# First feed-forward block of an encoder layer: high weights run once over both parts of the input, in another chunk order

## Chip, cores, metric

One NeuronCore of a Trainium2 chip runs the whole kernel. The metric is device time in microseconds (us). The kernel before takes 1095.23 us, the median of three runs.

## What is computed

One encoder layer over 256 tokens of width 2048: windowed attention, a normalisation, and a squared-ReLU network of hidden width 8192, each scaled and shifted by vectors that depend on a conditioning input `c`. The part at issue, cut from the reference:

```python
mod = c_act @ mod_w[i] + mod_b[i]
sh_m, sc_m, g_m, sh_f, sc_f, g_f = jnp.split(mod, 6, axis=-1)
...
hff = x * (1.0 + sc_f[:, None, :]) + sh_f[:, None, :]
u = jnp.square(jax.nn.relu(hff @ w1 + b1))
y = u @ w2 + b2
```

`x` here is the normalised output of the attention part; everything is float32.

## The kernel before

**Products in parts.** TensorE (PE) works on a reduced float32 format. So each operand is split: a high part (a copy in that format) and a low part (the rest). A product is the sum of three: high x high, high weights x low input, low weights x high input. For weights, ScalarE (ACT) makes the high part in L247 and VectorE (DVE) subtracts it from the raw weights in L218, for halves of 1024 columns. The class `Stream` plans all weight loads in one list, issues them on SyncE's queue (SP, L202) into five raw buffers, and keeps five high and five low buffers (`NHIGH`, `NLOW`). `S.main()` hands out the two halves of the next load, `S.done()` gives one half back and prepares further ones.

**The first feed-forward block.** The hidden width is worked off in four blocks of 2048. In blocks 1 to 3 (`ff_hidden`, L983) all 2048 rows of the input are at hand, and the high weights run over 512 columns, both input parts at once (L995), and the low weights over 256 (L996). In block 0 the input is still being made: the 16 slices of 128 rows come in four groups `h2[0]` to `h2[3]`. For that the first matrix is cut into 16 loads of 1 MB (`in_w1a`), here called tiles: tile (kg, fq) has the rows of input group kg and the quarter fq of the block's output columns; it holds 4 x 4 weight blocks of 128x128, that is four *quarters* `fi` of output columns with four slices k each. `W1A` (L470) is the order of the tiles; in that before, kg 0 of two fq, then kg 1 of the same two, and so on. The loop at L955 to L982 does, for each weight block, three products of 256 columns (L971 high x high, L972 high x low, L973 low x high); two quarters share a PSUM bank, one in each half. `psa` has five banks. After kg = 1 the sum of two groups is copied to SBUF by ACT (L977, `uacc`); after kg = 3 DVE adds the second half of the sum to it (L979), and `square_split` (L928) applies bias and ReLU (L934), squares (L936) and splits the result (L937, L938) for the second matrix.

**An input group.** `ff_columns(g)` (L879) needs the scale and shift for four slices: their matrix `in_modf` is multiplied by `c` partly on PE (L307), partly on DVE (L345), both as steps of the same stream; the last step adds the DVE part by PE (L307 with `onesf`), ACT copies the row (L361), two PE transposes (L377) turn it into columns, and DVE computes scale and shift vectors (L383, L384, L885 to L887). `ff_input(g)` (L896) then transposes `x` (L901, two PSUM tiles, two slices each), and for each slice ACT writes the high part (L907), ACT or DVE the full value (L910, L913), and DVE the low part (L915). Groups 1, 2 and 3 are made ahead of tiles 1, 7 and 9; they are used first in tiles 2, 8 and 10.

**Order.** Each engine runs its instructions in one order, which is settled when the kernel is built: a scheduler sorts the instructions as the loops emit them, by their dependences, and moves some past others. On an engine, an instruction that waits holds up what is behind it.

Of the kernel before, what the change touches and what calls it, by code (L numbers as in the profile page):

```python
# [11 lines left out]
F32 = mybir.dt.float32  # L12
F32R = mybir.dt.float32r
I32 = mybir.dt.int32
AF = mybir.ActivationFunctionType
# [5 lines left out]
S = 256  # L21
# [27 lines left out]
def hybrid_kernel(ctx: ExitStack, tc: tile.TileContext, a, out: bass.AP):  # L49
    nc = tc.nc  # L50
    cst = ctx.enter_context(tc.tile_pool(name="cst", bufs=1))
    sml = ctx.enter_context(tc.tile_pool(name="sml", bufs=4))
# [5 lines left out]
    psa = ctx.enter_context(tc.tile_pool(name="psa", bufs=5, space=PSUM))  # L58
# [7 lines left out]
    more = []  # L66
# [7 lines left out]
    def g4(dt=F32):  # L74
        return gen.tile([128, 1024], dt, tag="g4", name="g4")

    def f32(x):
        return x.bitcast(F32)
# [4 lines left out]
    cT, b1 = pack[:, :NK], pack[:, NK:NK + 64]  # L83
# [196 lines left out]
    S = Stream()  # L280
# [155 lines left out]
    for g in range(2, G):  # L436
        n = len(ORDER[g])
# [15 lines left out]
    def plan_late(n):  # L453
        for _ in range(n):
            while lp[0] < len(late) and late[lp[0]].planned == late[lp[0]].n:
                lp[0] += 1
            if lp[0] < len(late):
                late[lp[0]].plan()
# [8 lines left out]
            S.plan(a["wo"][(n - 5) % 4, (n - 5) // 4])  # L467
    S.stop = len(S.q)
    plan_late(4)
    W1A = [(kg, fq) for p in ((0, 1), (2, 3)) for q in ((0, 1), (2, 3)) for kg in p for fq in q]  # L470
    for n, (kg, fq) in enumerate(W1A):
        left = [m.n - m.planned for m, _, _ in m_ff]
        for _ in range(max(W1_FILL[n], left[2] if n == 6 else 0, left[2] + left[3] if n == 8 else 0)):
# [20 lines left out]
    def part(tiles, t, c):  # L494
        return tiles[c][:, t * 512:t * 512 + 512]
# [67 lines left out]
    def qkv(g, ch):  # L563

        _, k0, nk = m_mix[g]
        hh, hl = held[g]
        wh, wl = S.main()
        per = 4 // nk
        for ci in range(per):
            p = ch * per + ci  # L570
            c = CORD[p]
            go_on, held_back = c in half, ((g, ch), p) in CARRY
            pss = half.pop(c, None) or banks()
            for k2 in range(0, nk, 2):
                for t in range(NT):
                    for k in (k2, k2 + 1):
                        s = slice(k * 256 + t * 128, k * 256 + t * 128 + 128)
                        mm3(pss[t], hh[:, s], hl[:, s], wh(ci * nk + k), wl(ci * nk + k),
                            k == 0 and not go_on, k == nk - 1 and not held_back)
                S.done()  # L580
                if per == 1 and k2 == 0:
                    yield
            if held_back:
                half[c] = pss
            else:
                evict(c, pss)
            if per == 2 and ci == 0:
                yield
# [36 lines left out]
    for x, (g, c) in enumerate(qk_order):  # L625
        at = ORDER[g].index(c)
# [207 lines left out]
    for n in range(21):  # L834
        j, i = n // 4, n % 4
# [9 lines left out]
        if n + 1 < len(LATE):  # L845
            w = qkv(*LATE[n + 1])
        else:
            if n == 5:
                ys, bo = [g4b() for _ in range(4)], bias_all(a["bo"], [g4b(), g4b()])
            w = project((n - 5) // 4, (n - 5) % 4)  # L850
# [13 lines left out]
        if n == 9:  # L864

            for c in range(4):
                xs[c] = g4()
                i = nc.gpsimd.dma_start(xs[c].rearrange("p (t n) -> p t n", t=NT), a["x"][:, :, 512 * c:512 * c + 512])
# [12 lines left out]
    def ff_columns(g):  # L881
        m, k0, nk = m_ff[g]
        columns(m, modfb, (scf, shf), k0, nk)
        s = slice(k0, k0 + nk)
        nc.vector.tensor_mul(a2[:, s], lnT[:, 0, s], scf[:, s])  # L885
        nc.vector.tensor_mul(b2[:, s], lnT[:, 1, s], scf[:, s])
        nc.vector.tensor_add(b2[:, s], b2[:, s], shf[:, s])  # L887
# [6 lines left out]
    def ff_input(g):  # L894
        both, hf = [g4(F32R), g4(F32R)], g4()
        for kp in range(2):  # L896
            pt = pst.tile([128, 512], F32, name="pt")
            for i in range(2):
                k = 4 * g + 2 * kp + i
                for t in range(NT):  # L900
                    nc.tensor.transpose(pt[:, i * 256 + t * 128:i * 256 + t * 128 + 128],  # L901
                                        part(xs, t, k // 4)[:, (k % 4) * 128:(k % 4) * 128 + 128], ident)
            for i in range(2):
                k = 4 * g + 2 * kp + i
                s = slice((2 * kp + i) * 256, (2 * kp + i) * 256 + 256)
                hh, hl = (both[kp][:, i * 512 + x * 256:i * 512 + x * 256 + 256] for x in range(2))
                nc.scalar.activation(hh, pt[:, i * 256:i * 256 + 256], AF.Identity,  # L907
                                     scale=a2[:, k:k + 1], bias=b2[:, k:k + 1])
                if i:
                    nc.scalar.activation(hf[:, s], pt[:, i * 256:i * 256 + 256], AF.Identity,  # L910
                                         scale=a2[:, k:k + 1], bias=b2[:, k:k + 1])
                else:
                    nc.vector.tensor_scalar(hf[:, s], pt[:, i * 256:i * 256 + 256], a2[:, k:k + 1],  # L913
                                            b2[:, k:k + 1], op0=OP.mult, op1=OP.add)
                nc.vector.tensor_sub(hl, hf[:, s], f32(hh))  # L915
        return both

    def ff_in(k):

        return h2[k // 4][k % 4 // 2][:, k % 2 * 512:k % 2 * 512 + 512]  # L920

    h2 = [ff_input(0)]
# [2 lines left out]
            normed(c, t)  # L925


    def square_split(ps, ft, n, u, at):  # L928

        rl = sml.tile([128, 512], F32, name="rl", tag="t2", bufs=4)  # L930
        e = n * 256
        for i in range(n):
            s = slice(i * 256, i * 256 + 256)
            nc.scalar.activation(rl[:, s], ps[:, s], AF.Relu, bias=b1[:, ft + i:ft + i + 1])  # L934
        uf = sml.tile([128, 512], F32, name="uf", tag="t2", bufs=4)
        nc.vector.tensor_mul(uf[:, :e], rl[:, :e], rl[:, :e])  # L936
        nc.scalar.copy(u[:, at:at + e], uf[:, :e])  # L937
        nc.vector.tensor_sub(u[:, 512 + at:512 + at + e], uf[:, :e], f32(u[:, at:at + e]))  # L938

    def square_halves(ps, ft, u, at):  # L940

        v = sml.tile([128, 512], F32, name="rl", tag="t2", bufs=4)
        nc.scalar.activation(v[:, 256:], ps[:, 256:], AF.Identity, bias=b1[:, ft:ft + 1])
        nc.vector.tensor_add(v[:, :256], v[:, 256:], ps[:, :256])
        uf = sml.tile([128, 512], F32, name="uf", tag="t2", bufs=4)[:, :256]
        nc.vector.scalar_tensor_tensor(uf, v[:, :256], 0.0, v[:, :256], op0=OP.max, op1=OP.mult)
        h, l = u[:, at:at + 256], u[:, 512 + at:512 + at + 256]
        nc.scalar.copy(h, uf)
        nc.vector.tensor_sub(l, uf, f32(h))

    g2 = None
    uacc = [g4() for _ in range(4)]
    us = []
    opened = {}
    for n, (kg, fq) in enumerate(W1A):  # L955
        if n in (1, 7, 9):
            ff_columns(len(h2))
            h2.append(ff_input(len(h2)))
        wh, wl = S.main()
        for fp in range(2):  # L960
            if kg % 2 == 0:
                opened[fq, fp] = psa.tile([128, 512], F32, name="pa")
            ps = opened[fq, fp]
            for fi in range(2):
                o = ps[:, fi * 256:fi * 256 + 256]
                for k in range(4):
                    w = (fp * 2 + fi) * 4 + k
                    hb = ff_in(4 * kg + k)
                    hh, hl = hb[:, :256], hb[:, 256:]
                    new, end = kg % 2 == 0 and fi + k == 0, kg % 2 == 1 and fi == 1 and k == 3  # L970
                    nc.tensor.matmul(o, wh(w, 128), hh, start=new, stop=False)  # L971
                    nc.tensor.matmul(o, wh(w, 128), hl, start=False, stop=False)  # L972
                    nc.tensor.matmul(o, wl(w, 128), hh, start=False, stop=end)  # L973
            S.done()
            av = uacc[fq][:, fp * 512:fp * 512 + 512]
            if kg == 1:
                nc.scalar.copy(av, ps)  # L977
            elif kg == 3:
                nc.vector.tensor_add(av, av, ps)  # L979
                u = g4(F32R)  # L980
                square_split(av, fq * 4 + fp * 2, 2, u, 0)
                us.append(u)  # L982

    def ff_hidden(blk):
        nonlocal g2
# [40 lines left out]
    for blk in range(BLK - 1):  # L1026
        if blk:
            us = ff_hidden(blk)
# [18 lines left out]
    us = ff_hidden(blk)  # L1047
# [21 lines left out]
    for t in range(NT):  # L1069
        ps = psa.tile([128, 512], F32, name="pa")  # L1070
# [4 lines left out]
        for c in (1, 0, 2, 3):  # L1075
# [8 lines left out]
            q = nc.sync if c % 2 else nc.scalar  # L1084
# [91 lines left out]
```

## Time and profile before

| | us |
|---|---|
| median of three runs | 1095.23 |
| lowest and highest run | 1093.78, 1096.64 |
| profiled execution, first to last instruction (its span; what lies around it is not in the profile) | 1098.2 |
| block 0, first matrix (366.56 to 466.39 in the span) | 99.83 |

Times inside the span are from one profiled execution, whose span is 3.0 us above the median of the runs. Groups are named by line, engine and operation, with output and input names; "x256" is a count, and what follows the last bar is the time that the engine stood idle ahead of the group, with what ended it. In time-ordered lists the first two columns are start and duration in us. PE's recorded durations overlap each other.

### The profile page before, as it was taken

Reading aid. Unit: us, or ns where it says so; the run is one execution under the profiler, and the core shown is the slowest. Engines: PE = TensorE matmul, PEld = TensorE weight load, DVE = VectorE, ACT = ScalarE, POOL = GpSimd, SP = SyncE. Lnnn points to the kernel's source line nnn. Section 1 sums busy time; section 2 is a strip of 40 time slices with the busy share of each in tenths; the row PEclk is TensorE's granted clock in tenths of the full one; section 3 lists DMA queues with packets and bytes.
Section 4 is the critical chain, followed back from the end, with each engine's and each line's share of the span. In section 5 each row is a group of like instructions: output and inputs, shape, how many; then the busy total and the mean of one; then the engine's idle time right before and its main releaser. Section 6 shows DMA issues by size and latency. Waiting matters only on the chain.

```text
span 1098.2 us, 15487 instructions
## 1 busy us (share of the span) xinstructions
PE 1067.6 (97%) x6098; PEld 863.1 (79%) x6098; DVE 804.2 (73%) x1162; ACT 522.0 (48%) x806; POOL 30.0 (3%) x54
## 2 busy tenths in 40 slices
PE   8889999998999999999999999999999999999995
PEld 6657677665677799988888888888888888888884
DVE  4597899978899877754588889756666557665676
ACT  5333346765673537643344543344453334544340
POOL 1000000001000000000000010001000000000001
PEclk9989999999999999999999999999999999999998
DMA  9999987789985996555578788866555555557511
GB/s 384 425 427 425 427 357 280 271 297 379 377 315 201 361 360 244 185 192 192 195 301 303 272 313 306 312 220 225 184 189 190 197 196 186 178 185 267 191 75 77
DMA packets 43337, 292.70 MB, mean 267 GB/s; under 512 B 5104, under 2 KB 5232, under 8 KB 9472
## 3 DMA queue, kind: packets, MB, share of 16 engines
q1 hardware_dynamic: 39312, 279.85, 66.9%
q0 software_dynamic: 3200, 10.50, 2.7%
q10 hardware_dynamic: 752, 1.35, 0.3%
q8 instruction: 48, 0.79, 0.3%
q14 instruction: 25, 0.20, 0.0%
HBM read 289.57 MB, written 2.11 MB: 266 GB/s over the span
## 4 chain that ended last, share of the span: by engine, by line
PE 86%; DVE 7%; DMA 4%; ACT 2%; issue 1%; DVEq 0%; ACTq 0%
PE pa L995 16%; PE pa L500 15%; PE pa L498 15%; PE pa L499 15%; PE pa L996 8%; PE pa L972 3%; PE pa L971 3%; PE pa L973 3%; PE pm L307 3%; DVE wl L218 2%; DMA raw<-in_modm 2%; DMA raw<-in_modf 1%; DVE g L345 1%; DMA raw<-in_wqkv 1%; PE pa L687 1%; PE pa L743 1%
## 5 line engine op out<-in xcount | busy, mean ns | idle before, releaser
L218 DVE TENSOR_TENSOR wl<-raw,wh 128x1024 fp32r<-128x1024 f32 x332 | 403.9, 1223 | 223.6 <-ACT wh L247 222.9
L247 ACT CAST wh<-raw 128x1024 fp32r<-128x1024 f32 x332 | 347.1, 1051 | 441.3 <-PE pa L500 228.6
L498 PE MATMUL pa<-wh,g 128*128 128x512 f32 x816 | 324.1, 398 | 5.1 <-ACT g L519 2.6
L500 PE MATMUL pa<-wh,g 128*128 128x512 f32 x816 | 318.9, 392 | 4.1 <-DVE g L521 3.0
L499 PE MATMUL pa<-wl,g 128*128 128x512 f32 x816 | 320.0, 392 | 0.0
L995 PE MATMUL pa<-g,wh 128*128 128x512 f32 x768 | 270.1, 397 | 0.0
L996 PE MATMUL pa<-g,wl 128*128 128x256 f32 x768 | 214.9, 280 | 0.0
L498 PEld LDWEIGHTS pa<-wh,g 128*128 128x128 f32 x816 | 153.9, 189 | 46.8 <-issue 7.5
L500 PEld LDWEIGHTS pa<-wh,g 128*128 128x128 f32 x816 | 153.5, 188 | 41.2 <-DVE g L521 6.0
L499 PEld LDWEIGHTS pa<-wl,g 128*128 128x128 f32 x816 | 153.9, 189 | 33.0 <-issue 2.4
L995 PEld LDWEIGHTS pa<-g,wh 128*128 128x128 f32 x768 | 144.2, 188 | 36.0 <-issue 0.8
L996 PEld LDWEIGHTS pa<-g,wl 128*128 128x128 f32 x768 | 144.8, 189 | 0.1
L345 DVE SCALAR_TENSOR_TENSOR g<-raw,cact,g 128x1024 f32<-128x1024 f32 x65 | 82.6, 1280 | 2.8 <-DMA raw<-in_modf 2.3
L972 PE MATMUL pa<-g,wh 128*128 128x256 f32 x256 | 72.7, 285 | 0.4 <-DVE g L915 0.4
L971 PE MATMUL pa<-g,wh 128*128 128x256 f32 x256 | 72.5, 286 | 0.0
L973 PE MATMUL pa<-g,wl 128*128 128x256 f32 x256 | 72.3, 283 | 0.0
L307 PE MATMUL pm<-raw,cact 128*32 128x256 f32 (+2 forms) x776 | 48.8, 375 | 5.9 <-DMA raw<-in_modf 3.2
L971 PEld LDWEIGHTS pa<-g,wh 128*128 128x128 f32 x256 | 48.8, 192 | 1.3 <-issue 0.8
L972 PEld LDWEIGHTS pa<-g,wh 128*128 128x128 f32 x256 | 49.1, 192 | 0.9 <-DVE g L915 0.8
L973 PEld LDWEIGHTS pa<-g,wl 128*128 128x128 f32 x256 | 49.1, 192 | 0.0
L345 DVE SCALAR_TENSOR_TENSOR g4b<-raw,cact,g4b 128x1024 f32<-128x1024 f32 x32 | 40.7, 1280 | 9.0 <-DMA raw<-in_modgf 8.8
L307 PEld LDWEIGHTS pm<-raw,cact 128*32 128x32 f32 x776 | 20.9, 112 | 25.9 <-issue 11.5
(165 smaller groups left out, 741.6 us busy)
## 6 DMA issues: line engine op xcount, KB each, us to landing
raw<-in_w SPq DMA_DIRECT2D x64, 1024.0 KB, 4.9
raw<-in_w1b SPq DMA_DIRECT2D x48, 1024.0 KB, 5.0
raw<-in_modm SPq DMA_DIRECT2D x32, 1024.0 KB, 14.8
raw<-in_modf SPq DMA_DIRECT2D x32, 1024.0 KB, 6.9
raw<-in_wqkv SPq DMA_DIRECT2D x24, 1024.0 KB, 12.8
raw<-in_modgm SPq DMA_DIRECT2D x16, 1024.0 KB, 7.5
raw<-in_wo SPq DMA_DIRECT2D x16, 1024.0 KB, 7.5
raw<-in_w1a SPq DMA_DIRECT2D x16, 1024.0 KB, 7.6
```

Source lines behind the costliest of these rows:

```text
L218: self.pinned(nc.vector.tensor_sub(l, r, f32(self.hs[n])))
L247: self.pinned(nc.scalar.copy(h, s))
L307: i = nc.tensor.matmul(self.ps[32 * j:32 * j + 32, :w], lhsT[j] if type(lhsT) is list else lhsT, rhs[j], start=self.first, stop=stop)
L345: nc.vector.scalar_tensor_tensor(p[:, :e], s, cact[:, kt:kt + 1], p[:, :e], op0=OP.mult, op1=OP.add)
L498: nc.tensor.matmul(ps, xh, wh, start=start, stop=False)
L499: nc.tensor.matmul(ps, xh, wl, start=False, stop=False)
L500: S.prev = nc.tensor.matmul(ps, xl, wh, start=False, stop=stop).ins
L971: nc.tensor.matmul(o, wh(w, 128), hh, start=new, stop=False)
L972: nc.tensor.matmul(o, wh(w, 128), hl, start=False, stop=False)
L973: nc.tensor.matmul(o, wl(w, 128), hh, start=False, stop=end)
L995: nc.tensor.matmul(ps, wh(k, 128), hb, start=k == 0, stop=False)
L996: nc.tensor.matmul(ps[:, :256], wl(k, 128), hb[:, :256], start=False, stop=k == NK - 1)
```

## The change

The order of the tiles, the loop over them and the way results leave PSUM are changed; `square_split` goes, and `square_halves`, which blocks 1 to 3 use already, gets a further summand. A quarter of output columns now has a bank of its own: the high weights run over both input parts (512 columns, L957 of the new kernel), the low weights over the high part (256 columns, L958), and the two halves of the bank are summed when they leave it. After kg = 1 that is an ACT copy (L963) and a DVE add (L964); after kg = 3 it is `square_halves` with the sum of the first two groups added (L931 to L939). `W1A` now runs kg 0 and kg 1 of one fq in succession. Groups 1, 2 and 3 are made after the first quarter of tiles 0, 7 and 8, and are used first in tiles 1, 8 and 9.

```diff
-    W1A = [(kg, fq) for p in ((0, 1), (2, 3)) for q in ((0, 1), (2, 3)) for kg in p for fq in q]
+    W1A = [(kg, fq) for p in ((0, 1), (2, 3)) for fq in range(4) for kg in p]
...
-    def square_halves(ps, ft, u, at):
+    def square_halves(ps, ft, u, at, more=None):
...
         nc.vector.tensor_add(v[:, :256], v[:, 256:], ps[:, :256])
+        if more is not None:
+            nc.vector.tensor_add(v[:, :256], v[:, :256], more)
...
     for n, (kg, fq) in enumerate(W1A):
-        if n in (1, 7, 9):
-            ff_columns(len(h2))
-            h2.append(ff_input(len(h2)))
         wh, wl = S.main()
-        for fp in range(2):
+        for fi in range(4):
+            if fi == 1 and n in (0, 7, 8):
+                ff_columns(len(h2))
+                h2.append(ff_input(len(h2)))
             if kg % 2 == 0:
-                opened[fq, fp] = psa.tile([128, 512], F32, name="pa")
-            ps = opened[fq, fp]
-            for fi in range(2):
-                o = ps[:, fi * 256:fi * 256 + 256]
-                for k in range(4):
-                    w = (fp * 2 + fi) * 4 + k
-                    hb = ff_in(4 * kg + k)
-                    hh, hl = hb[:, :256], hb[:, 256:]
-                    new, end = kg % 2 == 0 and fi + k == 0, kg % 2 == 1 and fi == 1 and k == 3
-                    nc.tensor.matmul(o, wh(w, 128), hh, start=new, stop=False)
-                    nc.tensor.matmul(o, wh(w, 128), hl, start=False, stop=False)
-                    nc.tensor.matmul(o, wl(w, 128), hh, start=False, stop=end)
-            S.done()
-            av = uacc[fq][:, fp * 512:fp * 512 + 512]
+                opened[fi] = psa.tile([128, 512], F32, name="pa")
+            ps = opened[fi]
+            for k in range(4):
+                w = fi * 4 + k
+                hb = ff_in(4 * kg + k)
+                nc.tensor.matmul(ps, wh(w, 128), hb, start=kg % 2 == 0 and k == 0, stop=False)
+                nc.tensor.matmul(ps[:, :256], wl(w, 128), hb[:, :256], start=False, stop=kg % 2 == 1 and k == 3)
+            if fi % 2:
+                S.done()
+            av = uacc[fq][:, fi * 256:fi * 256 + 256]
             if kg == 1:
-                nc.scalar.copy(av, ps)
+                nc.scalar.copy(av, ps[:, 256:])
+                nc.vector.tensor_add(av, av, ps[:, :256])
             elif kg == 3:
-                nc.vector.tensor_add(av, av, ps)
-                u = g4(F32R)
-                square_split(av, fq * 4 + fp * 2, 2, u, 0)
-                us.append(u)
+                if fi % 2 == 0:
+                    us.append(g4(F32R))
+                square_halves(ps, fq * 4 + fi, us[-1], fi % 2 * 256, av)
```

More of the change, by code (lines that the diff above doesn't have):

```diff
@@ L925, in hybrid_kernel @@
             normed(c, t)
[L928 to L938, printed above, removed]
-    def square_halves(ps, ft, u, at):
+    def square_halves(ps, ft, u, at, more=None):
         v = sml.tile([128, 512], F32, name="rl", tag="t2", bufs=4)
```

## Prediction

> **What bounds the kernel now.** I read the page first, then busy time by stretch, then who waits for whom inside the changed stage, then the time-ordered lists of single engines there.
>
> ```profile
> span 1098.2 us, 15487 instructions
> ...
> PE 1067.6 (97%) x6098; PEld 863.1 (79%) x6098; DVE 804.2 (73%) x1162; ACT 522.0 (48%) x806; POOL 30.0 (3%) x54
> ```
>
> PE has matmuls in flight for 97% of the span. The changed stage runs from its first matmul, at 366.56 us, to the first of the second matrix, at 466.39. I cut it where tile 8, the first that needs input group 2, begins (columns: stretch; length; busy time and count of PE, PEld, DVE, ACT, POOL; granted clock; DMA share; GB/s):
>
> ```profile
> 366.56:419.23 52.67, 52.27 (x448) 49.63 (x446) 40.95 (x55) 28.41 (x41) 0.00 (x0) 1.00 0.95 373
> 419.23:466.39 47.16, 47.16 (x397) 47.16 (x396) 37.16 (x53) 31.63 (x49) 0.00 (x0) 1.00 0.56 201
> ```
>
> PE fills both parts at a granted clock of 1.00. Of the waits inside the stage, two matter:
>
> ```profile
> DVE wl L218 <- ACT wh L247: 16.7, 18, 1.7
> ...
> PE pa L972 <- DVE g L915: 0.4, 1, 0.4
> ```
>
> PE waited for an input part once, for 0.4 us; DVE waited 16.7 us for high halves, because it runs as far ahead as the five buffers allow. So the stage lasts as long as PE's own issue, and what PE gains or waits here moves the end by as much.
>
> **The matmuls.** A recorded duration overlaps its neighbours, so the price is the distance between starts. Here are two of the stage's 256-column products, the transposes L377 that begin group 2, and the first products of tile 8:
>
> ```profile
> 411.45 0.28 PE L972 MATMUL pa<-g,wh 128*128 128x256 f32 x1
> 411.57 0.28 PE L973 MATMUL pa<-g,wl 128*128 128x256 f32 x1
> 411.69 0.38 PE L377 MATMUL pt<-ident,mrow 128*128 128x128 f32 x2
> ...
> 419.23 0.52 PE L971 MATMUL pa<-g,wh 128*128 128x256 f32 x3
> ```
>
> The later blocks already run the new form, a 512-column and a 256-column product in turn. From the first to the last of these 18 starts of L995 are 17 pairs:
>
> ```profile
> 599.72 0.40 PE L995 MATMUL pa<-g,wh 128*128 128x512 f32 x1
> ...
> 605.73 0.40 PE L995 MATMUL pa<-g,wh 128*128 128x512 f32 x1
> ```
>
> Three narrow products take 3 x 0.12 = 0.360 us; a pair takes 6.01 / 17 = 0.3535 us. The stage has 16 tiles of 16 weight blocks, so 256 triples become 256 pairs: 256 x 0.0065 = **1.7 us gained**. A tile takes 5.66 instead of 5.76 us. That is all that halving the number of high-weight runs brings.
>
> **The evictions.** They cost DVE time, in single operations of these durations:
>
> ```profile
> L946 DVE SCALAR_TENSOR_TENSOR uf<-rl 128x256 f32<-128x256 f32 x27 | 11.4, 424 | 0.7
> L944 DVE TENSOR_TENSOR rl<-rl,pa 128x256 f32<-128x256 f32 x27 | 11.2, 416 | 0.6 <-ACT rl L943 0.5
> ...
> L979 DVE TENSOR_TENSOR g<-g,pa 128x512 f32<-128x512 f32 x8 | 5.5, 686 | 1.4 <-PE pa L973 1.3
> ```
>
> In the first half of the stage the eviction was a copy on ACT; now each of 16 quarters adds one 256-wide DVE add, 16 x 0.42 = 6.7 us. In the second half two quarters took three 512-wide operations (3 x 0.69); now each quarter takes four 256-wide ones: 64 x 0.42 - 24 x 0.69 = 10.3 us more. PE sees none of the first 6.7 us, since DVE had 52.67 - 40.95 = 11.7 us free there. In the second half 37.16 + 10.3 = 47.5 us stand against 47.16, so spacing decides:
>
> ```profile
> 590.00 0.42 DVE L944 TENSOR_TENSOR rl<-rl,pa 128x256 f32<-128x256 f32 x1
> 590.45 0.42 DVE L946 SCALAR_TENSOR_TENSOR uf<-rl 128x256 f32<-128x256 f32 x1
> ```
>
> An operation that needs the one before it starts 0.45 us after it. The list below gives 0.34 us between independent ones (419.82 to 420.16) and 1.15 for a weight split L218 (416.63 to 417.78). Two tiles then need 4 x 1.15 + 4 x (2 x 0.45 + 2 x 0.34) = 10.9 us of DVE against 11.31 of PE. I take 0.3 us of waits for a free bank (bounds 0 and, at full recorded durations, 1.2: the second rival).
>
> **The input groups, where I expect the loss.** The new chunk order runs both tiles of a quarter of the output columns in succession, so groups 1 and 3 are wanted one tile sooner than before, and their making is moved with them. The steps below follow the order of instructions on each engine in the changed kernel's build. DVE, before:
>
> ```profile
> 412.11 0.16 DVE L383 TENSOR_TENSOR scf<-pt,pack 128x4 f32<-128x4 f32 x1 [2.35 <-PE pt L377]
> 412.18 1.27 DVE L345 SCALAR_TENSOR_TENSOR g<-raw,cact,g 128x1024 f32<-128x1024 f32 x1
> ...
> 416.63 1.22 DVE L218 TENSOR_TENSOR wl<-raw,wh 128x1024 fp32r<-128x1024 f32 x1 [1.41 <-ACT wh L247]
> 417.78 0.54 DVE L913 TENSOR_SCALAR g<-pt,a,b 128x256 f32<-128x256 f32 x1
> 418.35 0.43 DVE L915 TENSOR_TENSOR g<-g,g 128x256 fp32r<-128x256 f32 x1
> ...
> 419.82 0.42 DVE L915 TENSOR_TENSOR g<-g,g 128x256 fp32r<-128x256 f32 x1
> 420.16 0.54 DVE L913 TENSOR_SCALAR g<-pt,a,b 128x256 f32<-128x256 f32 x1
> ...
> 422.27 0.42 DVE L915 TENSOR_TENSOR g<-g,g 128x256 fp32r<-128x256 f32 x1
> ...
> 424.94 0.43 DVE L915 TENSOR_TENSOR g<-g,g 128x256 fp32r<-128x256 f32 x1
> ```
>
> and ACT:
>
> ```profile
> 415.28 0.37 ACT L361 COPY mrow<-pm 128x256 f32<-128x256 f32 x1 [1.86 <-PE pm L307]
> 415.55 1.05 ACT L247 CAST wh<-raw 128x1024 fp32r<-128x1024 f32 x1
> 416.50 0.58 ACT L907 ACTIVATE g<-pt,b,a 128x256 fp32r<-128x256 f32 x1
> ```
>
> Group 2. All starts from L377, which DVE's L383 waits for. Before, the first low part is done 418.77 - 411.69 = 7.1 us after it and PE comes to tile 8 after 7.54, so 0.46 us are spare. Now L377 stands after the first quarter of tile 7 instead of ahead of it, so 12 pairs (4.24 us) and not 48 products (5.76) lie between: 1.52 us sooner. And DVE's path is longer. Behind L383 stand the add of a quarter that ACT has just copied, and two L345 instead of one; the last ends some 3.7 us after L377 (0.4 + 0.9 + two of 1.2). PE's L307 needs it, ACT's L361 needs L307 and starts after 4.4 instead of 3.6 us, and L247, L218, L913 and L915 follow in turn with one more add (0.36): 0.8 + 0.36 = 1.15 us. Wait: 1.52 + 1.15 - 0.46 = **2.2 us** (bounds 1.06, if the path doesn't grow, and 3.4, with one more split in it). The queues behind are what makes it long: L361 holds up every later L247 on ACT, and L218 stands ahead of L913 on DVE.
>
> Its third block. DVE needs two splits, two L915 and an L913 from the first low part to the third, 3.6 us with the wait for ACT; PE has two blocks of 4 x 0.3535 and L377, 3.0: **0.7 us** (0 to 1.2).
>
> Group 3. Before, 2.67 us lay between the last low part of group 2 and the first of group 3 (422.27, 424.94), and a whole tile of other work covered it. Now PE has the rest of tile 8 and a quarter of tile 10 that the order puts ahead, until some 4.25 us after group 2's last low part. DVE has two splits ahead of L913 whose high halves go into buffers that tile 8 itself frees: 1.45 (first half of tile 8 done) + 1.05 (L247) + 1.15 + 0.57 + 1.15 + 0.4 = 5.8 us. Wait: **1.5 us** (0 to 2.7, a split less or more).
>
> Group 1 I take at nothing: the order puts its four blocks one after the other across all four banks, 1.41 us of cover each, and DVE, a microsecond ahead at the start, makes one in about 1.6 (a split of 1.15 and an operation of 0.45); bounds 0 and 0.4, the wait that stands there already. The weight loads keep their order in SP's queue; POOL has nothing here.
>
> **Sum:** -1.7 + 2.2 + 0.7 + 1.5 + 0.3 = +3.0 us: the profiled execution's 1098.2 would become 1101.2. Its span is 0.27% above the median of the runs, 1095.23; a difference carries over, so I forecast **1098.2 us**, 0.27% up. About 0.3%, 3.3 us, can be told from no change.
>
> **Rivals.** *The inputs come in time.* PE keeps the 1.7 us: 1093.5. For it speaks that PE waited 0.4 us in the whole stage; against it, that only 0.46 us were spare at tile 8 and the order takes 1.52. Up to 1 us of wait belongs to this case.
>
> *DVE becomes the bound in tiles 9 to 15* (the other side). Five banks exist and four are open, so a late last read of one stops PE. At 10.9 of 11.31 us per two tiles DVE has 0.4 to spare. Each quarter needs ACT twice; if DVE stands idle for the length of just one narrow operation, 0.4 us, per quarter, it needs 12.5, 1.2 us too much, in 3.5 such pairs 4.2 us: 1102.4. It decides from 11.31 us on. Against it: the order puts splits between the dependent operations.
>
> *An instruction costs by itself, not by its columns.* By recorded means a pair would save 3 x 0.28 - 0.40 - 0.28 = 0.16 us, 41 us in all: 1054. The starts quoted above speak against it.
> The Trainium skill, TensorE: Matmul & The Clock Gate, section Back-to-back issue gap, has such a rule: in a stream with weight loads it gives some 81 ns for 128 columns and 131 for 512. An estimate from that page for 256 is 98 ns; a pair would save 65 ns, the stage 16.6 us, and the kernel would take 1078.6. This trace disagrees: 120 and about 234 ns.
>
> **How the numbers follow.** Forecast 0.63 (own range 1096.2 to 1100.5; two fifths of it above +3.3 us), inputs in time 0.13, DVE as bound 0.22, cost by instruction 0.02. Slower: 0.22 + 0.24 = 0.46; faster: 0.02 and a fifth of the second case, 0.05; within: 0.49. The range, 1093.0 to 1102.5, leaves out the upper half of DVE as bound, the last rival and what of the second would be faster still.
>
> **What would show it.** Pairs L957 to L957 0.35 us apart; PE waits for L915 of about 2 us ahead of tile 8 and 1.5 at tile 9, and none at tile 1; the stage about 103 us long. No wait at tile 8 makes me wrong downwards. Waits of PE for L932, or DVE without idle time after tile 9, make me wrong upwards, and so does a stage above 105 us.

## The result, and the profile after

The changed kernel takes 1099.41 us (median of 20 runs, 1096.12 to 1103.27) beside 1096.1 us before on the same chip (20 runs, 1093.78 to 1101.0). The ratio is **1.0024, 95% interval 1.0013 to 1.0034**: 1.4 to 3.7 us slower.

The page of the profiled execution (span; busy time, share and instructions of each engine):

```profile
span 1096.5 us, 15051 instructions
...
PE 1063.2 (97%) x5842; PEld 846.6 (77%) x5842; DVE 817.0 (75%) x1218; ACT 523.3 (48%) x822; POOL 30.0 (3%) x54
```

PE has 256 instructions less and DVE 56 more, as counted from the diff (16 + 64 - 24). This span is 1.7 us *shorter* than the one before, although the kernel is slower. The cause lies ahead of the changed stage: the last L307 of input group 0 starts at 361.76 us here and at 366.00 before. In the ten profiled experiments it starts anywhere from 361.1 to 364.6, whatever was changed behind it, while from the first product of the second matrix to the end of the span all twelve executions take between 631.7 and 631.9 us. So I compare **the stage**: from that L307 to that first product, L498. For the changed kernel:

```profile
361.76 0.63 PE L307 MATMUL pm<-g,onesf 128*32 128x256 f32 x6
363.29 0.47 PE L957 MATMUL pa<-g,wh 128*128 128x512 f32 x1 [0.90 <-ACT g L907]
...
464.65 0.39 PE L498 MATMUL pa<-wh,g 128*128 128x512 f32 x1
```

464.65 - 361.76 = 102.89 us; before it was 466.39 - 366.00 = 100.39. The stage is **2.5 us longer**, which agrees with the timed ratio. Busy time by stretch, cut again where tile 8 begins (stretch; length; PE, PEld, DVE, ACT, POOL; granted clock; DMA share; GB/s):

```profile
363.29:415.91 52.62, 50.78 (x317) 42.25 (x317) 44.29 (x68) 28.77 (x49) 0.00 (x0) 1.00 0.94 366
415.91:464.65 48.74, 46.88 (x266) 40.30 (x267) 43.85 (x84) 30.81 (x52) 0.00 (x0) 1.00 0.55 192
```

DVE has 10.0 us more to do than before (44.29 + 43.85 against 40.95 + 37.16), and PE now stands idle for 3.7 us of the two stretches together. The time-ordered list of PE says where; in square brackets stand the idle time and what ended it:

```profile
407.65 0.38 PE L377 MATMUL pt<-ident,mrow 128*128 128x128 f32 x2
...
411.36 0.64 PE L307 MATMUL pm<-g,onesf 128*32 128x256 f32 x8
...
415.91 0.47 PE L957 MATMUL pa<-g,wh 128*128 128x512 f32 x1 [1.84 <-DVE g L915]
...
419.48 0.47 PE L957 MATMUL pa<-g,wh 128*128 128x512 f32 x1 [0.30 <-DVE g L915]
...
426.35 0.47 PE L957 MATMUL pa<-g,wh 128*128 128x512 f32 x1 [1.53 <-DVE g L915]
```

These are the waits for group 2, for its third block and for group 3, forecast at 2.2, 0.7 and 1.5 us. There is no wait for a bank (L932) and none at tile 1. At the start PE waits 0.90 us: a 512-column product needs both parts at once, and the first low part is done at 363.14 (the L907 that the list names, of the next slice in the same tile, ends at 363.26). Before, PE started with the high part alone and waited 0.37 for the low one.

### The profile page after: what moved, and what is told of

Read it like the earlier page. It is cut to its first block, busy times and chain, and to the rows that moved or that the text cites. A ratio compares the mean times of both kernels' runs of the same rounds, so it can differ in the third digit from the quotient of the medians.

```text
span 1096.5 us, 15051 instructions
## 1 busy us (share of the span) xinstructions
PE 1063.2 (97%) x5842; PEld 846.6 (77%) x5842; DVE 817.0 (75%) x1218; ACT 523.3 (48%) x822; POOL 30.0 (3%) x54
## 4 chain that ended last, share of the span: by engine, by line
PE 83%; DVE 7%; DMA 6%; ACT 2%; issue 1%; DVEq 0%; SPq 0%; ACTq 0%
PE pa L981 16%; PE pa L500 15%; PE pa L498 15%; PE pa L499 15%; PE pa L982 8%; PE pa L957 5%; DMA raw<-in_modm 3%; PE pa L958 3%; DVE wl L218 2%; PE pm L307 2%; DVE g L345 2%; DMA raw<-in_wqkv 1%; DMA raw<-in_modf 1%; PE pa L687 1%; ACT wh L247 1%; PE pa L743 1%
## 5 line engine op out<-in xcount | busy, mean ns | idle before, releaser
L247 ACT CAST wh<-raw 128x1024 fp32r<-128x1024 f32 x332 | 347.1, 1052 | 422.6 <-PE pa L500 223.3
L498 PE MATMUL pa<-wh,g 128*128 128x512 f32 x816 | 322.9, 396 | 5.9 <-ACT g L519 2.9
L981 PE MATMUL pa<-g,wh 128*128 128x512 f32 x768 | 270.1, 397 | 0.0
L498 PEld LDWEIGHTS pa<-wh,g 128*128 128x128 f32 x816 | 153.1, 188 | 47.6 <-issue 7.4
L981 PEld LDWEIGHTS pa<-g,wh 128*128 128x128 f32 x768 | 144.2, 188 | 36.1 <-issue 0.8
L957 PE MATMUL pa<-g,wh 128*128 128x512 f32 x256 | 91.0, 400 | 4.6 <-DVE g L915 3.7
L345 DVE SCALAR_TENSOR_TENSOR g<-raw,cact,g 128x1024 f32<-128x1024 f32 x65 | 82.5, 1278 | 1.8 <-DMA raw<-in_modf 1.5
L958 PE MATMUL pa<-g,wl 128*128 128x256 f32 x256 | 70.4, 281 | 0.0
L957 PEld LDWEIGHTS pa<-g,wh 128*128 128x128 f32 x256 | 47.8, 188 | 17.1 <-ACT wh L247 2.1
L307 PE MATMUL pm<-raw,cact 128*32 128x256 f32 (+2 forms) x776 | 48.3, 373 | 5.6 <-DMA raw<-in_modf 2.9
L345 DVE SCALAR_TENSOR_TENSOR g4b<-raw,cact,g4b 128x1024 f32<-128x1024 f32 x32 | 40.7, 1280 | 14.1 <-DMA raw<-in_modgf 14.1
L958 PEld LDWEIGHTS pa<-g,wl 128*128 128x128 f32 x256 | 48.2, 188 | 1.4 <-issue 0.8
L307 PEld LDWEIGHTS pm<-raw,cact 128*32 128x32 f32 x776 | 21.0, 112 | 25.7 <-issue 12.1
L702 ACT ACTIVATE g<-pa,nm 128x256 f32<-128x256 f32 x64 | 29.5, 473 | 19.5 <-DVE nm L693 19.4
L537 DVE TENSOR_TENSOR g<-g,pa 128x512 f32<-128x512 f32 x42 | 27.5, 680 | 7.8 <-PE pa L500 7.7
```

What stands on the lines that cost most here:

```text
L247: self.pinned(nc.scalar.copy(h, s))
L307: i = nc.tensor.matmul(self.ps[32 * j:32 * j + 32, :w], lhsT[j] if type(lhsT) is list else lhsT, rhs[j], start=self.first, stop=stop)
L345: nc.vector.scalar_tensor_tensor(p[:, :e], s, cact[:, kt:kt + 1], p[:, :e], op0=OP.mult, op1=OP.add)
L498: nc.tensor.matmul(ps, xh, wh, start=start, stop=False)
L702: nc.scalar.activation(P[:, r * 256:r * 256 + 256], pss[r // 2][:, r % 2], AF.Exp, scale=-1.0, bias=nm[:, r:r + 1], accum_out=sm[:, r:r + 1])
L957: nc.tensor.matmul(ps, wh(w, 128), hb, start=kg % 2 == 0 and k == 0, stop=False)
```

## Experiments

The table gives for each kernel the stage, PE's waits in it (the idle times that the lists show, added up; start, groups, banks together), and the timed ratio. Stages and waits are from one profiled execution each.

| kernel | stage, us | waits, us | ratio to before (95%) |
|---|---|---|---|
| before | 100.39 | 0.37 | 1 |
| order_only | 100.91 | 0.37 | 0.9992 (0.9976 to 1.0007) |
| narrow_halves | 102.74 | 1.08 | 1.0012 (0.9997 to 1.0027) |
| changed kernel | 102.89 | 4.57 | 1.0024 (1.0013 to 1.0034) |
| after_again | 102.99 | 4.58 | 1.0023 (1.0010 to 1.0037) |
| no_first_add | 102.11 | 2.70 | 1.0017 (1.0001 to 1.0033) |
| group2_sooner | 103.00 | 3.11 | 0.9998 (0.9983 to 1.0013) |
| group3_ahead | 103.22 | 3.23 | 1.0019 (1.0002 to 1.0035) |
| one_more_add | 104.43 | 5.69 | 1.0036 (1.0022 to 1.0051) |
| act_square | 102.65 | 4.58 | 1.0026 (1.0012 to 1.0039) |
| both_and_start | 101.57 | 2.51 | 1.0012 (0.9998 to 1.0026) |
| act_square_all | 99.18 | 0.77 | 0.9985 (0.9973 to 0.9998) |

The second table cuts the stage into what PE does first to last: up to the end of its first sixteenth of the products, the next five sixteenths, four, and the last six. It is worked out from the starts of all products in PE's list, a 512-column product counted as two of 256. Groups 2 and 3 fall into the third column.

| kernel | start and 1st | 2nd to 6th | 7th to 10th | 11th to 16th |
|---|---|---|---|---|
| before | 9.88 | 30.05 | 25.90 | 34.56 |
| order_only | 9.98 | 29.98 | 26.39 | 34.56 |
| narrow_halves | 9.24 | 29.98 | 28.28 | 35.24 |
| changed kernel | 9.68 | 29.14 | 30.04 | 34.03 |
| both_and_start | 9.50 | 29.47 | 26.22 | 36.38 |
| act_square_all | 9.53 | 29.47 | 26.26 | 33.92 |

### Is one profile enough? (after_again)

The changed kernel, unedited. Expected:

> The changed kernel once more, on the chip of the two that follow. If the length of the stage in one profiled execution is a sound measure, it is again within 0.3 us of 102.89 us from the last L307 of group 0 to the first product of the second matrix, with the same three waits at tiles 8 and 9, though the span may differ by the 4 us that lie ahead of the stage; ratio 1.0013 to 1.0034 times before. Rival (single profiles scatter by a microsecond inside the stage, from half clock after a wait or otherwise): 103.5 us or more, or waits that differ by over 0.3 us.

Measured: 102.99 us, waits 1.84, 0.32 and 1.52 us at the same three places. The stage is a measure good to about 0.1 us, as long as PE's clock stays at 1.00 (see group2_sooner).

### The order alone (order_only)

```diff
-    W1A = [(kg, fq) for p in ((0, 1), (2, 3)) for q in ((0, 1), (2, 3)) for kg in p for fq in q]
+    W1A = [(kg, fq) for p in ((0, 1), (2, 3)) for fq in range(4) for kg in p]
...
-        if n in (1, 7, 9):
-            ff_columns(len(h2))
-            h2.append(ff_input(len(h2)))
...
             for fi in range(2):
+                if 2 * fp + fi == 1 and n in (0, 7, 8):
+                    ff_columns(len(h2))
+                    h2.append(ff_input(len(h2)))
```

(The diff is against before.) Expected:

> The kernel before (three 256-column products for each weight block, its copies and square_split) with only the tile order of the change and input groups 1, 2 and 3 made after the first quarter of tiles 0, 7 and 8. Theory (the later making of the groups costs the time, the products and evictions do not): no gain of matmuls, and PE waits for L915 ahead of tiles 8 and 9 as in the changed kernel, a little shorter since ACT alone evicts the first half: together 3 to 4.5 us, so 3 to 4.5 us slower than before, ratio 1.003 to 1.004, and no faster than the changed kernel. Rival (the four narrow evictions per quarter load DVE and make the groups late): waits at tiles 8 and 9 under 1 us together, ratio below 1.001.

Measured: no wait of PE for group 2 or 3 in the list, the stage 0.52 us longer. Most of that, 0.49 us, lies in the third column, in delays too short for the list: the product at 418.34 starts 0.42 us after the one before it, where 0.12 is usual, just behind the last low part of group 2. My theory falls, and the rival holds. The lists tell why. DVE and PE of order_only:

```profile
402.80 5.24 DVE L345 SCALAR_TENSOR_TENSOR g<-raw,cact,g 128x1024 f32<-128x1024 f32 x4
409.26 0.16 DVE L383 TENSOR_TENSOR scf<-pt,pack 128x4 f32<-128x4 f32 x1 [1.22 <-PE pt L377]
...
413.38 0.54 DVE L913 TENSOR_SCALAR g<-pt,a,b 128x256 f32<-128x256 f32 x1
413.95 0.42 DVE L915 TENSOR_TENSOR g<-g,g 128x256 fp32r<-128x256 f32 x1
```

```profile
408.84 0.38 PE L377 MATMUL pt<-ident,mrow 128*128 128x128 f32 x2
...
410.18 0.64 PE L307 MATMUL pm<-g,onesf 128*32 128x256 f32 x8
```

and DVE of the changed kernel at the same place:

```profile
408.06 0.16 DVE L383 TENSOR_TENSOR scf<-pt,pack 128x4 f32<-128x4 f32 x1 [1.06 <-PE pt L377]
408.25 0.42 DVE L964 TENSOR_TENSOR g<-g,pa 128x256 f32<-128x256 f32 x1
408.59 1.28 DVE L345 SCALAR_TENSOR_TENSOR g<-raw,cact,g 128x1024 f32<-128x1024 f32 x1
409.79 0.15 DVE L383 TENSOR_TENSOR shf<-pt,pack 128x4 f32<-128x4 f32 x1
409.90 1.28 DVE L345 SCALAR_TENSOR_TENSOR g<-raw,cact,g 128x1024 f32<-128x1024 f32 x1
...
411.18 0.41 DVE L964 TENSOR_TENSOR g<-g,pa 128x256 f32<-128x256 f32 x1
...
414.56 0.54 DVE L913 TENSOR_SCALAR g<-pt,a,b 128x256 f32<-128x256 f32 x1
415.01 0.41 DVE L964 TENSOR_TENSOR g<-g,pa 128x256 f32<-128x256 f32 x1
415.34 0.42 DVE L915 TENSOR_TENSOR g<-g,g 128x256 fp32r<-128x256 f32 x1
```

In order_only all four L345 have run by 408.04, while DVE would else have stood idle; L307 needs the last of them and starts 1.34 us after L377. In the changed kernel two L345 stand behind L383, that is behind a wait of 1.06 us for PE, with an add L964 between; L307 starts 3.71 us after L377. From L377 to the end of the first L915 it takes 414.37 - 408.84 = 5.5 us in order_only, 7.1 before, and 415.76 - 407.65 = 8.1 us in the changed kernel. Group 3 differs in the same way. ACT of order_only, then ACT and DVE of the changed kernel:

```profile
419.14 1.04 ACT L907 ACTIVATE g<-pt,b,a 128x256 fp32r<-128x256 f32 x2
420.69 1.05 ACT L247 CAST wh<-raw 128x1024 fp32r<-128x1024 f32 x1 [0.50 <-PE pa L972]
```

```profile
421.97 1.05 ACT L247 CAST wh<-raw 128x1024 fp32r<-128x1024 f32 x1 [2.36 <-PE pa L957]
422.93 0.56 ACT L907 ACTIVATE g<-pt,b,a 128x256 fp32r<-128x256 f32 x1
```

```profile
423.06 1.23 DVE L218 TENSOR_TENSOR wl<-raw,wh 128x1024 fp32r<-128x1024 f32 x1 [1.25 <-ACT wh L247]
424.20 0.54 DVE L913 TENSOR_SCALAR g<-pt,a,b 128x256 f32<-128x256 f32 x1
```

There L907 runs ahead of the L247 that waits for a buffer; here it stands behind one that waits 2.36 us, and L913 behind the split of that half.

### The evictions without the pairs (narrow_halves)

```diff
-                nc.tensor.matmul(ps, wh(w, 128), hb, start=kg % 2 == 0 and k == 0, stop=False)
+                nc.tensor.matmul(ps[:, :256], wh(w, 128), hb[:, :256], start=kg % 2 == 0 and k == 0, stop=False)
+                nc.tensor.matmul(ps[:, 256:], wh(w, 128), hb[:, 256:], start=False, stop=False)
```

Expected:

> The changed kernel with three 256-column products in place of each pair: high x high and low x high into the left half of the quarter's bank, high x low into the right half; tile order, evictions and places of the groups as in the changed kernel. In its build all four L345 stand ahead of the L383 of group 2 on DVE (in the changed kernel two stand behind it), while two splits still stand ahead of L913 of group 3. Theory (the order of DVE's queue sets the waits, and the adds L964 work through that order): PE's wait at tile 8 falls from 1.84 to 0.5 us or less, that at tile 9 stays between 1.0 and 1.6; matmuls cost 1.7 to 2.5 us more than the pairs; level with the changed kernel, 1.001 to 1.0025 times before. Rival (the narrow evictions make the groups late whatever the order): both waits as in the changed kernel, ratio 1.004 or more. Second rival (only PE's faster quarters expose the groups): no waits above 0.4 us, ratio 1.0005 or less.

Measured: 0.30 us of wait at tile 8, and not for the group but for an eviction (L965, the add of the changed kernel's L964), 0.78 at tile 9, ratio 1.0012. The theory of the queue order holds best; the wait at tile 9 is somewhat under its range. The path from L377 (410.56) to the end of the first L915 (417.76) is 7.2 us with the same load on DVE that takes 8.1 in the changed kernel. A narrow product can also begin with the high part alone, which is done earlier. With this kernel the 2.5 us of the stage can be split along a line of one-step changes: **the order +0.52 us, the evictions +1.83, the pairs +0.15**. By the second table the evictions cost 1.89 us in the third column and 0.68 in the fourth, and 0.74 are gained at the start. The last number is two large ones: the pairs gain 0.84 + 1.21 = 2.05 us in the second and fourth column, and lose 1.76 in the third and 0.44 at the start. A faster PE arrives earlier at inputs that come when DVE and ACT are done; but the path of group 2 is also 0.9 us longer in that build (8.1 against 7.2), and no run separates the two.

### The adds alone (no_first_add)

```diff
                 nc.scalar.copy(av, ps[:, 256:])
-                nc.vector.tensor_add(av, av, ps[:, :256])
```

Expected:

> The changed kernel without the DVE add L964 after kg = 1, so that the low part of the first half sum is left out of the result: 16 operations of 0.42 us less on DVE, ACT's copy and everything else as in the changed kernel. In its build L913 and L915 of group 2 stand ahead of two splits, those of group 3 still behind two. Theory (the adds bring the order in which group 2 is late): no wait for L915 at tile 8, 1.2 to 1.6 us of wait at tile 9; 2 us less than the changed kernel, ratio 1.000 to 1.001. Rival (group 2 is late because its transposes L377 come only 1.5 us sooner while it is wanted a tile earlier): tile 8 still waits 1 us or more, ratio 1.0015 or more.

Measured: no wait at tile 8, 1.58 us at tile 9 and 0.23 at a transpose. The waits are the theory's; but the stage is only 0.78 us shorter, not 2, and the ratio, 1.0017, is above the theory's range. DVE in this kernel:

```profile
411.75 0.55 DVE L913 TENSOR_SCALAR g<-pt,a,b 128x256 f32<-128x256 f32 x1 [0.64 <-PE pm L307]
412.33 0.42 DVE L915 TENSOR_TENSOR g<-g,g 128x256 fp32r<-128x256 f32 x1
413.13 2.36 DVE L218 TENSOR_TENSOR wl<-raw,wh 128x1024 fp32r<-128x1024 f32 x2 [0.38 <-ACT wh L247]
415.41 0.42 DVE L915 TENSOR_TENSOR g<-g,g 128x256 fp32r<-128x256 f32 x1
```

The two splits that stood ahead of the group now stand in it, and PE runs into gaps in place of one wait: of the 2.0 us saved at tile 8 (9.68 to 7.64 us for the eighth sixteenth), 0.95 come back in the next (7.33 to 8.28). So a second thing is at work: what is put behind the group is late instead.

### Each group by itself (group2_sooner, group3_ahead)

```diff
-            if fi == 1 and n in (0, 7, 8):
+            if fi == 1 and n in (0, 6, 8):
```

> The changed kernel with input group 2 made after the first quarter of tile 6 instead of tile 7. Theory: PE's waits for L915 at tile 8 (1.84 and 0.30 us) go, the one at tile 9 (1.53 us, group 3 behind two weight splits) stays; about 2 us less than the changed kernel, level with before (ratio to before 1.000 to 1.001). Rival (DVE and ACT have no room for the group wherever it stands): a wait of the same size for L915 or for a low half L218 appears within tiles 6 to 9 and the time stays at 1.0024 times before.

Measured: the waits at tile 8 are gone; the one at tile 9 is 2.21 us instead of 1.53; the time is level with before (0.9998), as the theory had it, though not the longer wait. The profiled stage, 103.00 us, doesn't show that gain. The busy time by stretch of this kernel says why (the granted clock is the third column from the end):

```profile
422.80:425.00 2.20, 0.04 (x1) 0.00 (x0) 2.20 (x5) 1.37 (x4) 0.00 (x0) 1.00 0.94 339
425.00:428.40 3.40, 3.36 (x10) 2.90 (x11) 1.05 (x3) 1.08 (x3) 0.00 (x0) 0.50 0.32 135
428.40:432.00 3.60, 3.60 (x22) 3.14 (x22) 2.59 (x5) 2.19 (x4) 0.00 (x0) 1.00 0.00 0
```

After the wait PE ran 3.4 us at a granted clock of 0.50, half of which, 1.7 us, is lost by estimate. More on it in the last section.

For group 3, with a wrapper (`S.pinned`) around L907, L910, L913 and L915 that keeps an instruction in the order of the loops while `S.pin` is set:

```diff
+        S.pin = n == 8
         wh, wl = S.main()
...
-                nc.vector.tensor_sub(hl, hf[:, s], f32(hh))
+                S.pinned(nc.vector.tensor_sub(hl, hf[:, s], f32(hh)))
```

> The changed kernel with the instructions that make group 3 (L907, L910, L913, L915) held in the order in which the loops emit them relative to the weight halves, so that DVE's L913 and L915 of group 3 stand ahead of the splits instead of behind two of them. Theory: the wait for a weight buffer that tile 8 frees is what delays group 3, so PE's wait at tile 9 falls from 1.53 us to under 0.4, that at tile 8 stays at 1.8; 1.1 to 1.5 us less than the changed kernel, ratio to before about 1.001. Rival (PE then waits for the splits that were put back): a wait for L218 of the same size in tiles 9 to 11, time unchanged at 1.0024.

Measured: no wait for group 3, 1.84 us at tile 8 as before, and 0.49 us in two waits for L932 that were not there; PE ran at half clock here too, for 3.4 us after tile 8's wait (about 1.7 us lost). The last six sixteenths take 35.1 us instead of 34.0. Theory and rival both hold a part: the wait goes, and about 1 us comes back as later DVE work. The ratio, 1.0019, can't be told from 1.0024.

### DVE's reserve (one_more_add, act_square)

```diff
             nc.vector.tensor_add(v[:, :256], v[:, :256], more)
+            nc.vector.tensor_add(more, more, more)
```

> The changed kernel with one further 256-column add on DVE per quarter in the tiles with kg = 3 (it doubles the saved half sum after its use, work that the layer does not need): 16 adds of 0.42 us. By the spacing in the prediction DVE then needs 10.9 + 4 x 0.45 = 12.7 us per two tiles against 11.31 of PE. Theory (the changed kernel stood just under DVE's limit): DVE becomes the bound, PE waits for L932 or L218 after tile 9, 3 to 5 us more than the changed kernel, ratio to before 1.005 to 1.007. Rival (DVE still has room, since its spacing estimate was too high): no PE waits for banks or halves, time within 0.7 us of the changed kernel.

Measured: 1.54 us more, all of it in the last six sixteenths, with 1.06 us of waits for L932. Neither side is right. 16 operations of 0.42 us are 6.7 us; 1.5 of it reached PE. DVE was not at its limit, but had less than 6.7 us to spare.

The reverse, with one operation less on DVE and one more on ACT:

```diff
-        nc.scalar.activation(v[:, 256:], ps[:, 256:], AF.Identity, bias=b1[:, ft:ft + 1])
-        nc.vector.tensor_add(v[:, :256], v[:, 256:], ps[:, :256])
-            nc.vector.tensor_add(v[:, :256], v[:, :256], more)
-        nc.vector.scalar_tensor_tensor(uf, v[:, :256], 0.0, v[:, :256], op0=OP.max, op1=OP.mult)
...
+            nc.vector.scalar_tensor_tensor(v[:, :256], ps[:, :256], b1[:, ft:ft + 1], more, op0=OP.add, op1=OP.add)
+            nc.vector.tensor_add(v[:, :256], v[:, :256], ps[:, 256:])
+            nc.scalar.activation(v[:, :256], v[:, :256], AF.Relu)
+            nc.scalar.activation(uf, v[:, :256], AF.Square)
```

(for kg = 3 alone; blocks 1 to 3 keep the old form)

> The changed kernel with a lighter eviction in the tiles with kg = 3: DVE adds the bias, the left half and the saved sum in one operation and the right half in a second, ACT does ReLU and square, so DVE has three 256-column operations per quarter instead of four and ACT three instead of two. The groups are made where they are in the changed kernel. Theory (in the changed kernel DVE still had a reserve after tile 9; the loss lies at tiles 8 and 9, ahead of the first of these evictions): waits at tiles 8 and 9 unchanged, stage within 0.6 us of the changed kernel, ratio 1.0015 to 1.003. Rival (DVE's load after tile 9 costs PE time all along): the stage is 1 us or more shorter, ratio 1.0015 or less.

Measured: waits unchanged, stage 0.24 us shorter, ratio 1.0026: the theory. In the changed kernel as it is, DVE's load after tile 9 costs PE next to nothing.

### The causes removed together (both_and_start, act_square_all)

both_and_start takes the edits of group2_sooner and group3_ahead and

```diff
+                if n == 0 and fi == 0:
+                    nc.tensor.matmul(ps[:, :256], wh(w, 128), hb[:, :256], start=k == 0, stop=False)
+                    nc.tensor.matmul(ps[:, 256:], wh(w, 128), hb[:, 256:], start=False, stop=False)
+                else:
+                    nc.tensor.matmul(ps, wh(w, 128), hb, start=kg % 2 == 0 and k == 0, stop=False)
```

> The changed kernel with group 2 made after the first quarter of tile 6, group 3's instructions held in their order ahead of the splits that follow, and three 256-column products in the first quarter of tile 0, which let PE begin with the high part alone. Theory (the three waits are separate, each has its own cause): no wait of PE for L915 at tiles 8 and 9 above 0.4 us, the start as before, so the stage takes 99.0 to 99.6 us against 100.4 before; 1 us faster than before, ratio 0.9985 to 0.9995, some 3.5 us less than the changed kernel. Rival (one lateness is passed on: what is put behind the groups, the splits and evictions, is then late): a wait of 1 us or more for L218, L932 or L915 in tiles 8 to 11, ratio 1.0005 or more.

Measured: the groups cost 0.32 us, and the third column falls by 3.8 us, to within 0.4 us of before. But the stage falls by 1.32 only, since the fourth column rises by 2.35. PE's waits in it:

```profile
PE pa L962 <- DVE rl L932: 1.7, 3, 0.7
PE pm L307 <- DMA raw<-in_modf: 1.1, 1, 1.1
PE pa L960 <- DVE g L915: 0.5, 1, 0.5
PE pa L962 <- DVE g L915: 0.3, 1, 0.3
```

(waits; total, times, longest; the second one lies ahead of the stage). The rival holds in kind: 1.7 us for L932, though in three waits of at most 0.72 us from the twelfth sixteenth on, later than it said. The splits behind the groups have become DVE work for the time after tile 9, where DVE would now be the bound. If that is so, the lighter eviction of act_square, which gained 0.24 us by itself, must be worth far more here. All edits together:

> The same lighter eviction, together with group 2 made after the first quarter of tile 6, group 3's instructions ahead of the splits, and three 256-column products in the first quarter of tile 0. Theory (the splits put behind the groups are DVE work that has to be done later, and came back as waits for L932 since DVE had no reserve): with 16 operations of 0.42 us less on DVE the waits for the eviction in tiles 10 to 15 go, 1.7 us or more, and the stage takes 98.8 to 100.0 us against 101.6 without the lighter eviction and 100.4 before; ratio 0.9985 to 1.000. Rival (the waits for L932 come from ACT, which has more to do now): waits for the eviction stay at 1.5 us or more, ratio 1.001 or more.

Measured: no wait for the eviction left, stage 99.18 us, 2.39 less than without the lighter eviction, ratio 0.9985 (0.9973 to 0.9998). The theory holds: the waits are gone, and stage and ratio lie in its ranges. This version has the pairs of the changed kernel and is faster than both kernels, than before by little (the interval ends at 0.9998). PE's waits and busy time over the stage in it:

```profile
PE pa L964 <- DVE g L915: 0.5, 1, 0.5
PE pa L966 <- DVE g L915: 0.3, 1, 0.3
```

```profile
361.69:460.30 98.61, 97.84 (x590) 83.04 (x588) 84.17 (x140) 65.48 (x113) 0.00 (x0) 1.00 0.78 295
```

PE is again busy nearly throughout (97.84 of 98.61 us), with DVE at 84.17 us and ACT at 65.48.

## Why the prediction came out right, and which step of it was wrong

The forecast was +3.0 us; the timed ratio gives +2.6 (0.0024 x 1096.1), the stage +2.5. (The median of 1099.41 us lies 1.2 above the forecast of 1098.2, and before's own median came out 0.9 higher with 20 runs than with three.) In the stage, PE's listed waits grew by 4.20 us (4.57 against 0.37) where 4.7 were forecast, and all the rest got 1.7 us shorter, as forecast. There is luck in that: group 2, its third block and the banks together came out 1.06 us below the forecast, and a wait of 0.53 us at the start was not foreseen. Step by step:

- **Matmuls** (1.7 us gained): right in kind, sized somewhat low. Pairs with nothing between them are mostly 0.343 to 0.361 us apart, and a sixteenth without anything else takes 5.54 to 5.65 us instead of 5.76; the pairs gained 2.05 us in the second and fourth column, 11 of the 16 sixteenths, where 1.7 x 11/16 = 1.2 were forecast. The rival by which an instruction costs by itself is out.
- **Group 2** (2.2), **third block** (0.7), **group 3** (1.5): measured 1.84, 0.30 and 1.53 us. The paths were as worked out: for group 2 the last L345 delays L307 and L361, and for group 3 L915 stands behind two splits (423.06 and 424.65), of which the first waits for a half that tile 8 frees. The third block came out at less than half.
- **Start** (nothing): a wait of 0.90 us instead of 0.37. That a 512-column product needs both input parts was overlooked. With the shorter products behind it the first sixteenth still ended 0.2 us sooner; the three narrow products there gained 0.2 us more in both_and_start (9.50 against 9.68).
- **Banks** (0.3): no wait in the list. The last six sixteenths took 34.03 us, where six undisturbed ones of 5.55 would take 33.3; what the shorter delays between them wait for is open. The spacing estimate, 10.9 of 11.31 us per two tiles, was too tight: one_more_add was to cost 3 to 5 us by it and cost 1.5.
- **The evictions of the first half** (nothing): this is **the step that failed**: "PE sees none of the first 6.7 us, since DVE had 52.67 - 40.95 = 11.7 us free there". The free time was an average over the stretch. Some of the adds stand in the microseconds in which group 2 is made, and in the build with them two L345 stand behind the wait of L383 and two splits ahead of L913. (Two of these adds I had counted myself, in the path of group 2.) And the loss that I put down to the new order, 1.52 us of time taken where 0.46 were to spare, doesn't come with the order alone: order_only has no listed wait for either group, as its path from L377 shrank from 7.1 to 5.5 us. I took the path of before as given and added to it. It is set by the order on DVE and ACT, which every edit rearranges. So the sum was right for this kernel, whose own order of instructions I had read, while the cause was put down to the wrong part: the order alone costs 0.5 us, the evictions 1.8, and the pairs' gain is lost in the same waits.

The rival of DVE as bound in tiles 9 to 15 did not happen here (act_square: 0.24 us), but is the next limit: it took most of the gain of both_and_start.

What the scheduler weighs when it puts two L345 ahead of L383 in one build and behind it in another stays open. That the place in the queue counts is shown by narrow_halves, with the same load, all L345 ahead and no wait for group 2, and by no_first_add, in which two splits have changed places with the group. Neither place alone made group 2 late: in no_first_add two L345 stand behind L383 too (at 408.18 and 409.49), and the first L915 still ends 5.1 us after L377 (407.61 to 412.76); in narrow_halves two splits stand ahead of L913 too (414.19 to 416.64). In the changed kernel both come together. But narrow_halves has a slower PE and no_first_add less work as well, and a build that differs from the changed kernel in the place of the L345 or of the splits alone was not run.

## What to carry to other kernels

Free time of an engine, averaged over a stage, covers an added operation only where that operation does not fall into a short chain that PE will wait for; look at the queue order in those few microseconds, in the build of the changed kernel. When a part of the work is moved ahead on a nearly full engine, ask what it is moved ahead of: here three waits of 3.7 us together vanished by such moves, and most of it came back 10 to 40 us later, until the engine itself got less to do. Split a change of several parts into builds that add one part at a time: the gain of the pairs was real (2 us), and only the sum of the parts hid it.

## What the runs showed of the hardware

A wait can cost more than its length. In group3_ahead the wait at tile 8 was 1.84 us, the same as in the changed kernel, after_again, one_more_add and act_square. In those PE went on at a clock of 1.00; in group3_ahead the granted clock fell to 0.50 for 3.4 us soon after the wait (busy time by stretch, columns as above; the mean of 0.82 in the second row means that 0.4 of its 1.2 us were at 0.50):

```profile
416.00:417.70 1.70, 0.00 (x0) 0.00 (x0) 1.70 (x5) 1.70 (x4) 0.00 (x0) 1.00 0.95 328
417.70:418.90 1.20, 1.15 (x6) 1.11 (x7) 1.20 (x2) 1.20 (x4) 0.00 (x0) 0.82 0.79 259
418.90:421.90 3.00, 3.00 (x11) 2.51 (x10) 2.92 (x8) 2.54 (x4) 0.00 (x0) 0.50 0.75 265
```

and the pairs of PE were 421.32 - 420.68 = 0.64 us apart instead of 0.35:

```profile
420.68 0.63 PE L958 MATMUL pa<-g,wh 128*128 128x512 f32 x1
421.10 0.41 PE L959 MATMUL pa<-g,wl 128*128 128x256 f32 x1
421.32 0.63 PE L958 MATMUL pa<-g,wh 128*128 128x512 f32 x1
```

The same happened after the 2.21 us of group2_sooner. The Trainium skill, TensorE: Matmul & The Clock Gate, section Why this matters for your kernels, puts the limit for such a fall at gaps of more than about 3 us; here a gap of 1.84 us (415.91 to 417.75) was enough, in one of five executions with that gap.

The Trainium skill, TensorE: Matmul & The Clock Gate, section What's actually happening, says that the activity is counted in free-running windows; then it depends on where in a window a gap falls. The clocks of the twelve traces agree with that: in each, all changes of the granted clock lie whole multiples of 3.413 us apart. Cut into steps of that grid, the twelve spans have 3791 steps at full clock. All 27 in which PE's records are idle for 56% or more were followed by a step at half clock, so were 5 of the 23 with 43 to 54%, and none with less. The 1.84 us of group3_ahead lie within one step and make up 54% of it; in the changed kernel, after_again and one_more_add the gap is split between two steps, and the fuller one has 38, 35 and 47%. In group2_sooner it is 63%. In act_square the gap lies within one step as well, 54%, and no fall followed: what decides near one half stays open. The Trainium skill, TensorE: Matmul & The Clock Gate, section Back-to-back issue gap, gives N / 1.2 ns for a product of N columns at half clock, so 427 + 213 = 640 ns for a pair, which is an estimate from that page; the trace agrees, with 0.64 us.
